# Crossing from the up projection to the down projection: where four activation blocks are loaded, and in which order the down projection's loads are issued

## Chip, cores and metric

The kernel runs on one core of a Trainium2 chip. The metric is the device time of one execution in microseconds (us). A core has five engines, each with its own instruction stream: TensorE (PE, matrix products into PSUM banks), VectorE (DVE), ScalarE (ACT), GpSimd (POOL) and SyncE (SP, here only a queue that issues DMAs). ACT issues some DMAs as well. Engines wait for one another by semaphores; within a stream instructions go in order.

## The reference

One layer of a streaming encoder on 1088 tokens (1024 of a prompt and 64 of a running stream): a mixer of latent attention and gated linear attention, a residual, and then the multilayer perceptron, with which this change has to do:

```python
h2 = rms_norm(x, g_norm2) * (1 + scale2) + shift2
x = x + gate2 * (jnp.square(jax.nn.relu(h2 @ w_up)) @ w_down)
```

`w_up` is 1024 x 4096, `w_down` 4096 x 1024, all in float32.

## The kernel before

**Arithmetic.** Both projections are done as seven products of half-size blocks in place of eight (a Strassen scheme). The seven products are numbered 0 to 6; the four blocks of a matrix are named 11, 12, 21 and 22. Each float32 operand is split into a high and a low part (`split`, lines 100 to 102: ACT casts the high part at L101, another engine, mostly DVE, subtracts it to get the low part at L102), and a product is three matmuls: high by high, high by low, low by high (`mm3`, lines 91 to 95).

**Up projection** (`up`, from line 1531). The 2048 rows of a half are done in 16 blocks of 128 (`j`). Block `j` has seven products of two token halves (272 columns each) and twelve matmuls per half, in the order 0, 1, 2, 5, 3, 4, 6 from `j` = 2 on. ReLU and square are applied and the seven activation combinations that the down projection needs are stored to DRAM (`keep_act`, line 1526), as `u_d[product, j]`, each 128 x 544 floats (272 KB). The stores of block 15 are issued by ACT, those of all others by SP. The activation tiles `st` come from a pool of six places, `sq_`, used in turn; the sums and differences are tiles `sc` from a pool of two places. `AH[j]` and `AL[j]` hold the split token operands of the up products; the places of `AH[0]`, `AL[0]`, `AH[1]`, `AL[1]` carry the tags `ah0`, `al0`, `ah1`, `al1` and outlive the stage.

**Down projection** (`down`, from line 1737). The products come in the order 0, 2, 3, 6, 1, 5, 4, each in 16 steps `(i, j)`, 112 steps in all. A step is 24 matmuls of 272 columns (four row blocks, two token halves, three matmuls) and needs an operand set `opers`: the split weights W (128 x 512) and the split activations U (128 x 544). There are four places for sets: `ah1`, `al1`, and two in the stage's own pool, so the set of step n can be made only when step n-4 is done. W comes out of a quad, four steps' weights in one load of 1 MB (`load_quad`, L1614); U is one 272 KB load of `u_d[i, j]` (`load_u`, L1619) into a ring of eight tiles `ru` that lies where the `st` tiles were. The first four sets need quad (11, 0) and `u_d[0, 0]` to `u_d[0, 3]`. Product 2 uses W = 12 - 22 + 11, so DVE makes 16 differences (`differences`, L105) and 16 sums (L1724) before it; `residual` (L1687) loads four residual blocks `e`, to which `out` (L1776) adds the products.

**What sets the order.** The program text is written by `interleave` (line 46): several generators run against a counted time, and the first in the list that is able goes on. In the up stage the list is `norm2, weights, tokens, up, ahead`; `ahead` (line 1629) writes the first loads and splits of the down projection. Its list in the down stage is `loads, operands, differences, down`. `loads` (line 1680) names, for each quad and residual, the step after which it is written; `PLACES` (line 1669) says where each quad lies. The compiler's scheduler then puts each engine's instructions in order by readiness, in a model of the machine, and may issue a load before others written ahead of it. `tc.keep_in_program_order(x)` takes this freedom away: x is issued behind the instruction that was written before it for the same engine.

Of the kernel before, what the change touches and what calls it, by code (L numbers as in the profile page):

```python
# [10 lines left out]
F32 = mybir.dt.float32  # L11
# [8 lines left out]
P = 128  # L20
# [11 lines left out]
HT = TOK // 2  # L32
# [39 lines left out]
def layer(ctx: ExitStack, tc: tile.TileContext, I, O):  # L72
# [149 lines left out]
    def has(*keys):  # L222
        return lambda: all(k in done or k in groups for k in keys)
# [1164 lines left out]
    with ExitStack() as uctx:  # L1388
# [9 lines left out]
        sq_ = pool("sq", 6)  # L1398
# [212 lines left out]
        def load_quad(x, q, t):  # L1611
            kh, nh = x // 10 - 1, x % 10 - 1
            r0 = 16 * P * kh + 4 * P * q
            SP.dma_start(t, I["w_down"][r0:r0 + 4 * P, 512 * nh:512 * nh + 512].rearrange("(j p) n -> p j n", p=P))  # L1614
            for j in range(4):
                quads[x, 4 * q + j] = t[:, j]

        def load_u(i, j, t, eng=SP):
            eng.dma_start(t, u_d[i, j])  # L1619
            ru[i, j] = t  # L1620

        def split_set(i, j, o, w):

# [5 lines left out]
        def ahead():  # L1629

            yield 0, 0, has("p 15 0")
            for j in range(2):
                load_u(0, j, sq_.tile([P, HT], F32, name="st"), ACT)
            load_quad(11, 0, keep.tile([P, 4, 512], F32, name="quad", tag="ah0"))
            yield 0, 0, has("p 15 1")
            load_quad(11, 1, keep.tile([P, 4, 512], F32, name="quad", tag="al0"))
            yield 0, 3000, None
            for j in range(2):
                split_set(0, j, keep.tile([P, D + TOK], F32R, name="opers", tag=("ah1", "al1")[j]), quads[11, j])
                yield 0, 1000, None  # L1640
# [5 lines left out]
    with ExitStack() as dctx:  # L1646

        PRODUCTS = (0, 2, 3, 6, 1, 5, 4)  # L1650
        STEPS = [(i, j) for i in PRODUCTS for j in range(16)]
        def pool(name, bufs=1):
            return dctx.enter_context(tc.tile_pool(reuse_waits="tile", name=name, bufs=bufs))

        ep = pool("ep")
        E = [ep.tile([P, 4, HT], F32, name=f"e{i}") for i in range(4)]
        rp = pool("rp", 8)
        sp_ = pool("sp")
        def new_quad(n):

            if n in ("x11", "x12"):
                return keep.tile([P, 4, 512], F32, name="quad", tag=n)
            return qp_.tile([P, 4, 512], F32, name="quad", tag=f"quad{n}")

        for _ in range(8):
            rp.tile([P, HT], F32, name="ru")
        opers = [sp_.tile([P, D + TOK], F32R, name="opers", tag=f"set{n}") for n in range(2)]
        qp_ = pool("qp_")
        PLACES = {11: (None, None, 3, 4), 12: (5, 6, 7, 8), 22: (0, 1, 2, "x11"), 21: (5, 6, 7, 8)}
        for n in range(9):  # L1670
            qp_.tile([P, 4, 512], F32, name="quad", tag=f"quad{n}")

        PLACE = {"22": (1, 4), "11": (0, 0), "12": (0, 4), "21": (1, 0)}

        ADDS = {0: ("11", False), 2: ("12", False), 3: ("22", False), 6: ("21", True), 1: ("22", True), 5: ("12", True),
                4: ("11", True)}
        OUT = {c: E[n] for n, c in enumerate(("11", "12", "22", "21"))}
        SPANS = ((0, 0, 512), (1, 512, HT))

        def loads():  # L1680

            def quad(x, q):
                load_quad(x, q, new_quad(PLACES[x][q]))

            def residual(c):
                th, m0 = PLACE[c]
                SP.dma_start(OUT[c], x2_d[:, m0:m0 + 4, HT * th:HT * th + HT])  # L1687

            quad(11, 2)
            for (i, j), what in (((0, 1), (11, 3)), ((0, 3), (12, 0)), ((0, 4), (22, 0)), ((0, 6), "11"), ((0, 8), (12, 1)),  # L1690
# [3 lines left out]
                yield 0, 0, has(f"dn {i} {j}")  # L1694
                if isinstance(what, str):
                    residual(what)
                else:
                    quad(*what)

        def differences():  # L1700

            for j in range(16):
                yield 0, 600, lambda: (12, j) in quads and (22, j) in quads
                sub(quads[12, j], quads[22, j], quads[12, j], DVE)
                done.add(f"diff {j}")

        def operands():
            n_u = 2
            part = {}
            for n, (i, j) in enumerate(STEPS):  # L1710
                while n_u < len(STEPS) and n_u < n + 7:
                    load_u(*STEPS[n_u], rp.tile([P, HT], F32, name="ru"))
                    n_u += 1
                if n < 2:
                    continue
                if n == 2:
                    yield 0, 2500, None
                if n >= 4:
                    yield 0, 600, has("dn %d %d" % STEPS[n - 4])
                x = {0: 11, 2: 11, 3: 12, 6: 21, 1: 11, 5: 22, 4: 21}[i]  # L1720
                yield 0, 0, lambda: (x, j) in quads and (i != 2 or f"diff {j}" in done)
                w = quads[x, j]
                if i == 2:
                    DVE.tensor_tensor(out=w, in0=w, in1=quads[12, j], op=ALU.add)  # L1724
                elif i == 6:
                    if j % 4 == 0:
                        part["t4"] = new_quad("x12")
                    w = part["t4"][:, j % 4]
                    sub(w, quads[21, j], quads[11, j], DVE)
                elif i == 1:  # L1730
                    sub(w, quads[22, j], w, DVE)
                o = (keep.tile([P, D + TOK], F32R, name="opers", tag=("ah1", "al1")[n % 4]) if n % 4 < 2 else
                     sp_.tile([P, D + TOK], F32R, name="opers", tag=f"set{n % 4 - 2}"))
                split_set(i, j, o, w)
                yield 0, 1500, None

        def down():
            banks = {}
            for i in PRODUCTS:
                if i in (0, 1, 4):  # L1740
                    banks.clear()
                late = (14, 15) if i == 4 else (15,)
                for j in range(late[0]):
                    yield 0, 0, lambda: (i, j) in sets
                    for m in range(4):
                        for h in range(2):
                            part(banks, i, j, m, h)
                            yield 375, 0, None
                    done.add(f"dn {i} {j}")
                for m in range(4):  # L1750
                    for h in range(2):
                        for j in late:
                            yield 0, 0, lambda: (i, j) in sets
                            part(banks, i, j, m, h)
                            yield 375, 0, None
                        out(i, m, h, banks[m, h])
                for j in late:
                    done.add(f"dn {i} {j}")

        def part(banks, i, j, m, h):  # L1760
            if (m, h) not in banks:
                banks[m, h] = bank()[:, 0:HW]
            wh, wl, uh, ul = sets[i, j]
            ms, hs = slice(m * P, m * P + P), HALVES[h]
            first = i in (0, 1, 4)
            mm3(banks[m, h], wh[:, ms], wl[:, ms], uh[:, hs], ul[:, hs], first and j == 0, j == 15, not first)

        def out(i, m, h, b):

            c, end = ADDS[i]  # L1770
            th, m0 = PLACE[c]
            e = OUT[c][:, m]
            for s, c0, c1 in SPANS:
                c0, c1 = max(c0, h * HW), min(c1, h * HW + HW)
                if c0 < c1:
                    DVE.scalar_tensor_tensor(out=e[:, c0:c1], in0=b[:, c0 - h * HW:c1 - h * HW],  # L1776
                                             scalar=modT[:, 5, m0 + m, s:s + 1], in1=e[:, c0:c1], op0=ALU.mult, op1=ALU.add)
            if h and end:
                SP.dma_start(O["y_T"][(m0 + m) * P:(m0 + m + 1) * P, HT * th:HT * th + HT], e)

        interleave([loads(), operands(), differences(), down()])


# [60 lines left out]
```

## Time and profile before

| | us |
|---|---|
| three runs: lowest, median, highest | 1432.69, 1434.76, 1436.42 |
| the profiled execution, its own time | 1434.8 |
| its span, first to last instruction | 1433.0 |
| PE busy | 1354.2 (95%) |
| DVE busy | 873.9 (61%) |
| ACT busy | 655.5 (46%) |

The profile gives, for one execution, what every engine did when. "Busy" of PE counts a matmul at whatever clock it ran at. In a timeline each row is a start, a duration, an engine and a line, and in brackets the idle time ahead of it and what ended that. A wait on several things is put down to the last. The granted clock (PEclk) is a share of TensorE's full 2.4 GHz.

### The profile page before, as it was taken

The page shows a single profiled execution, that of the slowest core. Times are in us where ns is not written, and L with a number is a line of the kernel's source. Part 1 is how long each engine was busy: PE and PEld are TensorE (multiplying, and loading weights), DVE is VectorE, ACT ScalarE, POOL GpSimd, SP SyncE. Part 2 cuts the span into 40 slices and gives each one's busy share as a digit, 9 for nine tenths or more (in the row PEclk, how much of TensorE's full clock was granted, in tenths as well). Part 3 has the DMA queues.
Part 4 walks back from the last instruction along what each step waited for, and adds up shares of the span by engine and source line. Part 5 has one row for each costly group of instructions (what it writes and reads, how often), then busy time and mean ns, then how long its engine had stood idle before and what let it go on. Part 6 is the DMA issues. An engine that isn't in the chain of part 4 may idle for free.

```text
span 1433.0 us, 26460 instructions
## 1 busy us (share of the span) xinstructions
PE 1354.2 (95%) x10014; PEld 1268.7 (89%) x10014; DVE 873.9 (61%) x1894; ACT 655.5 (46%) x1623; POOL 273.1 (19%) x388
## 2 busy tenths in 40 slices
PE   6988899978999999999979999999997999999998
PEld 5887778877866779899968999999996999999998
DVE  5688787236455756645399566556533866774554
ACT  5455554334335666644365444444433343334332
POOL 3255445113131211014663000000000000000000
PEclk9999999999999999999988999999998999999999
DMA  9320021474244441264315444444248945433441
GB/s 347 103 71 9 16 80 49 134 210 120 87 141 131 141 130 59 70 188 130 113 32 172 147 155 138 133 152 152 96 159 301 340 135 157 148 116 104 126 124 38
DMA packets 165594, 188.17 MB, mean 131 GB/s; under 512 B 16814, under 2 KB 116442, under 8 KB 165466
## 3 DMA queue, kind: packets, MB, share of 16 engines
q1 hardware_dynamic: 157722, 180.34, 39.6%
q10 hardware_dynamic: 7744, 6.13, 1.3%
q8 instruction: 79, 1.29, 0.4%
q14 instruction: 49, 0.40, 0.1%
HBM read 132.97 MB, written 53.46 MB: 130 GB/s over the span
## 4 chain that ended last, share of the span: by engine, by line
PE 76%; DVE 10%; DMA 5%; ACT 3%; POOL 3%; issue 2%; SPq 0%; DVEq 0%; ACTq 0%; POOLq 0%
PE mm L93 13%; PE mm L94 13%; PE mm L95 13%; PE g L93 5%; PE g L95 5%; PE g L94 5%; PE mm L964 3%; PE tp L93 3%; PE tp L95 3%; PE tp L94 3%; PE g L991 2%; PE mm L166 2%; DMA raw<-in_w_in 1%; PE tp L1001 1%; DMA gv<-mix_d 1%
## 5 line engine op out<-in xcount | busy, mean ns | idle before, releaser
L101 ACT CAST opers<-quad 128x512 fp32r<-128x512 f32 x112 | 69.5, 620 | 191.6 <-PE mm L95 176.8
L102 DVE TENSOR_TENSOR opers<-quad,opers 128x512 fp32r<-128x512 f32 x112 | 77.2, 689 | 116.0 <-ACT opers L101 116.0
L93 PE MATMUL mm<-opers 128*128 128x272 f32 x448 | 128.9, 289 | 9.9 <-ACT opers L101 9.9
L95 PE MATMUL mm<-opers 128*128 128x272 f32 x448 | 129.7, 290 | 0.0
L94 PE MATMUL mm<-opers 128*128 128x272 f32 x448 | 129.3, 289 | 0.4 <-DVE opers L102 0.4
L93 PE MATMUL mm<-ah,wh 128*128 128x272 f32 x424 | 123.7, 293 | 6.2 <-ACT st L1565 6.2
L95 PE MATMUL mm<-ah,wl 128*128 128x272 f32 x424 | 123.5, 292 | 1.1 <-POOL wl L102 1.1
L94 PE MATMUL mm<-al,wh 128*128 128x272 f32 x424 | 123.5, 292 | 0.0
L93 PEld LDWEIGHTS mm<-opers 128*128 128x128 f32 x448 | 85.0, 190 | 10.4 <-ACT opers L101 10.4
L93 PE MATMUL mm<-hh,wh 128*128 128x384 f32 (+2 forms) x264 | 90.7, 347 | 0.5 <-ACT hh L101 0.5
L94 PE MATMUL mm<-hl,wh 128*128 128x384 f32 (+2 forms) x264 | 87.7, 333 | 0.0
L93 PEld LDWEIGHTS mm<-ah,wh 128*128 128x128 f32 x424 | 82.0, 194 | 6.4 <-ACT st L1565 6.4
L95 PE MATMUL mm<-hh,wl 128*128 128x384 f32 (+2 forms) x264 | 87.2, 331 | 0.0
L94 PEld LDWEIGHTS mm<-opers 128*128 128x128 f32 x448 | 84.8, 189 | 0.6 <-DVE opers L102 0.6
L95 PEld LDWEIGHTS mm<-opers 128*128 128x128 f32 x448 | 85.1, 190 | 0.0
L95 PEld LDWEIGHTS mm<-ah,wl 128*128 128x128 f32 x424 | 81.4, 192 | 1.3 <-POOL wl L102 1.3
L94 PEld LDWEIGHTS mm<-al,wh 128*128 128x128 f32 x424 | 81.7, 193 | 0.0
L102 DVE TENSOR_TENSOR opers<-ru,opers 128x544 fp32r<-128x544 f32 x110 | 79.0, 719 | 1.0 <-ACT opers L101 0.9
L101 ACT CAST wh<-ru 128x512 fp32r<-128x512 f32 x67 | 41.2, 619 | 70.9 <-PE g L94 26.0
L101 ACT CAST opers<-ru 128x544 fp32r<-128x544 f32 x110 | 70.6, 643 | 4.5 <-PE mm L95 3.6
L93 PE MATMUL mm<-wh,hh 128*128 128x264 f32 (+3 forms) x216 | 65.8, 305 | 1.6 <-ACT wh L213 1.6
L94 PE MATMUL mm<-wl,hh 128*128 128x264 f32 (+3 forms) x216 | 64.8, 300 | 1.0 <-DVE wl L105 0.9
(415 smaller groups left out, 4436.0 us busy)
## 6 DMA issues: line engine op xcount, KB each, us to landing
ru<-u_d SPq DMA_DIRECT2D x110, 272.0 KB, 2.7
raw<-in_w_ada SPq DMA_DIRECT2D x40, 512.0 KB, 3.8
ru<-in_w_up SPq DMA_DIRECT2D x32, 512.0 KB, 4.0
quad<-in_w_down SPq DMA_DIRECT2D x16, 1024.0 KB, 5.8
u_d<-st SPq DMA_DIRECT2D x60, 272.0 KB, 2.1
u_d<-sc SPq DMA_DIRECT2D x45, 272.0 KB, 2.2
raw<-in_w_in SPq DMA_DIRECT2D x22, 256.0 KB, 3.3
x<-in_xo_T SPq DMA_DIRECT2D x8, 544.0 KB, 5.0
```

Of the source, the lines that this page charges most:

```text
L93: PE.matmul(out, lhsT=ah, rhs=bh, start=first, stop=False, skip_group_check=more)
L94: PE.matmul(out, lhsT=ah, rhs=bl, start=False, stop=False, skip_group_check=more)
L95: PE.matmul(out, lhsT=al, rhs=bh, start=False, stop=last, skip_group_check=more)
L101: ACT.copy(hi, src)
L102: eng.tensor_tensor(out=lo, in0=src, in1=f32(hi), op=ALU.subtract)
L166: mm = PE.matmul(acc[32 * j:32 * j + 32, 0:256], lhsT=scT[:, k, :], rhs=was[k][:, 256 * j:256 * (j + 1)], start=(k == 0), stop=(k == KT - ...
L964: PE.matmul(sp[:n, :w], lhsT=x[:, hd, :n], rhs=y[:, hd, :w], start=(j == 0), stop=(j == 4))
L991: PE.matmul(op[:n, 0:P], lhsT=pt[:kw, k, :n], rhs=kvs[kt // 4].v[:kw, kt % 4, hd], start=(kt == 0), stop=(kt == nkt - 1))
L1001: PE.transpose(tp[:kw, k, :n], pr[k0 // 4][:n, P * k:P * k + kw], ident[:n, :n])
```

## The change

`load_quad` and `load_u` return the DMA. `ahead` no longer loads U of the first two steps by ACT into `st` tiles; it loads U of the first four by SP into the four quarters of one tile `u4` in the place `al0`, right behind quad (11, 0). Quad (11, 1), which lay in `al0`, goes to place 3, (11, 2) to place 4, and (11, 3) to `al0` after `u4`. All other loads of the down projection are kept in program order, and some are written after other steps than before. The ring of `ru` starts with step 4, and the counted pause of 2500 ahead of the split of step 2 goes.

```diff
         def load_quad(x, q, t):
             kh, nh = x // 10 - 1, x % 10 - 1
             r0 = 16 * P * kh + 4 * P * q
-            SP.dma_start(t, I["w_down"][r0:r0 + 4 * P, 512 * nh:512 * nh + 512].rearrange("(j p) n -> p j n", p=P))
+            dma = SP.dma_start(t, I["w_down"][r0:r0 + 4 * P, 512 * nh:512 * nh + 512].rearrange("(j p) n -> p j n", p=P))
             for j in range(4):
                 quads[x, 4 * q + j] = t[:, j]
-
-        def load_u(i, j, t, eng=SP):
-            eng.dma_start(t, u_d[i, j])
+            return dma
+
+        def load_u(i, j, t):
             ru[i, j] = t
+            return SP.dma_start(t, u_d[i, j])
...
             yield 0, 0, has("p 15 0")
-            for j in range(2):
-                load_u(0, j, sq_.tile([P, HT], F32, name="st"), ACT)
             load_quad(11, 0, keep.tile([P, 4, 512], F32, name="quad", tag="ah0"))
-            yield 0, 0, has("p 15 1")
-            load_quad(11, 1, keep.tile([P, 4, 512], F32, name="quad", tag="al0"))
-            yield 0, 3000, None
+            u4 = keep.tile([P, 4, HT], F32, name="u4", tag="al0")
+            for j in range(4):
+                load_u(0, j, u4[:, j])
+            yield 0, 3000, has("p 15 1")
...
-            if n in ("x11", "x12"):
+            if n in ("x11", "x12", "al0"):
                 return keep.tile([P, 4, 512], F32, name="quad", tag=n)
...
-        PLACES = {11: (None, None, 3, 4), 12: (5, 6, 7, 8), 22: (0, 1, 2, "x11"), 21: (5, 6, 7, 8)}
+        PLACES = {11: (None, 3, 4, "al0"), 12: (5, 6, 7, 8), 22: (0, 1, 2, "x11"), 21: (5, 6, 7, 8)}
...
             def quad(x, q):
-                load_quad(x, q, new_quad(PLACES[x][q]))
+                tc.keep_in_program_order(load_quad(x, q, new_quad(PLACES[x][q])))
 
             def residual(c):
                 th, m0 = PLACE[c]
-                SP.dma_start(OUT[c], x2_d[:, m0:m0 + 4, HT * th:HT * th + HT])
-
-            quad(11, 2)
-            for (i, j), what in (((0, 1), (11, 3)), ((0, 3), (12, 0)), ((0, 4), (22, 0)), ((0, 6), "11"), ((0, 8), (12, 1)),
-                                 ((0, 10), (22, 1)), ((0, 13), (12, 2)), ((0, 15), (22, 2)), ((2, 2), (12, 3)),
+                tc.keep_in_program_order(SP.dma_start(OUT[c], x2_d[:, m0:m0 + 4, HT * th:HT * th + HT]))
+
+            quad(11, 1)
+            for (i, j), what in (((0, 1), (11, 2)), ((0, 4), (11, 3)), ((0, 5), (12, 0)), ((0, 6), (22, 0)), ((0, 7), "11"),
+                                 ((0, 9), (12, 1)),
+                                 ((0, 11), (22, 1)), ((0, 13), (12, 2)), ((0, 15), (22, 2)), ((2, 2), (12, 3)),
                                  ((2, 4), (22, 3)), ((2, 7), "12"), ((2, 12), "22"), ((3, 3), (21, 0)), ((3, 7), (21, 1)),
                                  ((3, 11), (21, 2)), ((3, 15), (21, 3)), ((6, 4), "21")):
...
         def operands():
-            n_u = 2
+            n_u = 4
             part = {}
             for n, (i, j) in enumerate(STEPS):
                 while n_u < len(STEPS) and n_u < n + 7:
-                    load_u(*STEPS[n_u], rp.tile([P, HT], F32, name="ru"))
+                    tc.keep_in_program_order(load_u(*STEPS[n_u], rp.tile([P, HT], F32, name="ru")))
                     n_u += 1
                 if n < 2:
                     continue
-                if n == 2:
-                    yield 0, 2500, None
```

## Rows read from the trace of the kernel before

**Rows 1.** Stretches: length, busy (instructions) of PE, PEld, DVE, ACT, POOL; clock, DMA.
```profile
1059.40:1080.30 20.90, 20.90 (x168) 20.79 (x167) 7.33 (x14) 8.14 (x17) 0.00 (x0) 1.00 0.62 213
1080.30:1100.60 20.30, 10.00 (x50) 9.44 (x50) 6.83 (x11) 3.10 (x5) 0.00 (x0) 0.66 1.03 384
...
1110.00:1160.00 50.00, 50.00 (x404) 50.00 (x403) 44.73 (x78) 19.62 (x34) 0.00 (x0) 1.00 0.86 302
1160.00:1400.00 240.00, 240.00 (x1930) 240.00 (x1930) 143.25 (x252) 94.02 (x161) 0.00 (x0) 1.00 0.41 125
```

**Rows 2.** Waits of PE from 1030 us on: total, times, longest.
```profile
PE mm L93 <- ACT opers L101: 9.9, 2, 8.4
```

**Rows 3.** Timeline of PE at the crossing.
```profile
1080.12 0.29 PE L95 MATMUL g<-ah,wl 128*128 128x272 f32 x1
1088.80 1.05 PE L93 MATMUL mm<-opers 128*128 128x272 f32 x3 [8.39 <-ACT opers L101]
...
1095.37 0.39 PE L93 MATMUL mm<-opers 128*128 128x272 f32 x1 [1.54 <-ACT opers L101]
...
1100.59 0.29 PE L93 MATMUL mm<-opers 128*128 128x272 f32 x1
```

**Rows 4.** Timeline of ACT and its DMA issues (ACTq) at the crossing.
```profile
1067.86 0.62 ACT L101 CAST opers<-quad 128x512 fp32r<-128x512 f32 x1 [0.26 <-DMA quad<-in_w_down]
...
1077.73 0.61 ACT L101 CAST opers<-quad 128x512 fp32r<-128x512 f32 x1
...
1079.74 0.33 ACTq L1529 DMA_DIRECT2D u_d<-sc  x1
1080.16 0.40 ACTq L1619 DMA_DIRECT2D st<-u_d  x1
...
1087.14 0.33 ACTq L1529 DMA_DIRECT2D u_d<-sc  x1
1087.56 0.50 ACTq L1619 DMA_DIRECT2D st<-u_d  x1
1088.11 0.64 ACT L101 CAST opers<-st 128x544 fp32r<-128x544 f32 x1 [8.70 <-DMA st<-u_d]
```

**Rows 5.** Timeline of SP's DMA issues (SPq) at the crossing.
```profile
1062.61 0.99 SPq L1614 DMA_DIRECT2D quad<-in_w_down  x2
1077.31 0.98 SPq L1614 DMA_DIRECT2D quad<-in_w_down  x2
1086.81 0.37 SPq L1614 DMA_DIRECT2D quad<-in_w_down  x1
1087.82 0.34 SPq L1619 DMA_DIRECT2D ru<-u_d  x1
```

**Rows 6.** Timeline of DVE at the crossing.
```profile
1081.24 0.43 DVE L1551 TENSOR_TENSOR st<-st,g 128x272 f32<-128x272 f32 x1
...
1086.38 0.73 DVE L105 TENSOR_TENSOR sc<-st 128x544 f32<-128x544 f32 x1 [3.48 <-DMA u_d<-sc]
```

**Rows 7.** DMA issues by line, whole span: count, KB each, median us to landing.
```profile
ru<-u_d SPq DMA_DIRECT2D x110, 272.0 KB, 2.7
...
quad<-in_w_down SPq DMA_DIRECT2D x16, 1024.0 KB, 5.8
...
u_d<-sc SPq DMA_DIRECT2D x45, 272.0 KB, 2.2
```

**Rows 8.** Operations on the tiles `ru` and `quad`: shortest, median, longest in ns.
```profile
L101 ACT CAST opers<-ru x110: 637/643/649, 1096.6 to 1418.0; 128x544 fp32r<-128x544 f32 x110
L102 DVE TENSOR_TENSOR opers<-ru,opers x110: 714/718/727, 1097.2 to 1418.7; 128x544 fp32r<-128x544 f32 x110
...
L105 DVE TENSOR_TENSOR quad<-quad x48: 680/683/693, 1112.8 to 1270.7; 128x512 f32<-128x512 f32 x48
```

**Rows 9.** Waits in SP's queue from 1030 us on: total, times, longest.
```profile
SPq L1779 <- DVE e L1776: 37.6, 13, 29.6
...
SPq L1614 <- PE mm L95: 13.7, 1, 13.7
```

## The prediction

> **What bounds the kernel now.** I looked first at stretches of the span, then at what PE waits for in the last third, then at the timelines around that place, engine by engine. The stretches say where there is something to gain. In the last up block PE does 168 matmuls in 20.90 us, 124.4 ns each, at the full clock; from 1110 us to 1400 us it is busy without a gap at the full clock; between them lie 20.30 us with only 50 matmuls, a mean clock of 0.66 (between the levels of 1.2 and 2.4 GHz) and the DMA engines full [rows 1]. PE's waits from 1030 us on come to 9.9 us in two pieces, for ACT's casts of `opers` [rows 2]. So the down projection is bound by PE except at its start, and only there can a change of loads win.
>
> The timeline of PE gives the price of the crossing. The last up matmul starts at 1080.12, so the next could start at 1080.24; step 2 of the down projection starts at 1100.59, after the 48 matmuls of steps 0 and 1 [rows 3]. These take 48 x 0.1244 = 5.97 us at the full clock. 1100.59 - 1080.24 - 5.97 = **14.4 us lost**: 8.6 us until step 0, 1.7 us between steps 0 and 1, and the rest, about 4.1 us, by matmuls at the lower clock after the pauses and a short wait for a low part.
>
> Why the two operands are late stands in ACT's timeline. W of step 0 is cast at 1067.86, 12 us ahead of time. U is loaded at 1080.16 for step 0 and at 1087.56 for step 1, each right behind a store of block 15 [rows 4], although block 0 of `u_d` was written long before. The code explains it: `up` stands ahead of `ahead` and is nearly always able, so the loads are written after all of block 15, and their `st` tiles are taken in turn after that block's last; the second stands in ACT's stream behind the store of the last difference, which ACT can issue only at 1087.14, since DVE waited until 1086.38 for a place of `sc` to be stored [rows 4, 6]. Each load then shares the DMA engines with four 1 MB quads issued by SP from 1077.31 to 1086.81 [rows 4, 5], and the cast waits 8.70 us [rows 4].
>
> **The change, part by part.**
> - *U of steps 0 to 3 in `al0`.* The place comes free with the first product of block 15: the two quads that before went to `ah0` and `al0` were issued from 1062.61 on [rows 5]. Now it is one quad and 4 x 0.28 MB, about as much data, so I take the same time. A quad lands in 5.8 us, a U load in 2.7 us in the median [rows 7]; queued behind one another they should be there by about 1070. Cast and subtraction take 0.64 + 0.72 us for each U [rows 8]; ACT and DVE are busy 8.14 and 7.33 of 20.90 us in that block [rows 1]. Sets 0 and 1 are then whole by some 1073, 7 us before PE wants them. Price on PE: nothing; without this cover, each us of lateness costs one.
> - *What was on ACT.* Two issues of 0.40 and 0.50 us go [rows 4], and SP gets two more (0.34 us each [rows 5]). ACT's casts no longer stand behind loads.
> - *Steps 2 and 3.* Their W was cast from 1077.73 on [rows 4], their U can follow at once. Step 2 is due at 1080.24 + 2.99 = 1083.2 + 2.99 = 1086.2. Bound from above: its U stands on ACT behind the store of the last difference. Without four quads in flight that difference need not wait until 1086.38: stores of `sc` take 2.2 us [rows 7] after 1079.74 [rows 4], so about 1083, and U is whole by 1085.5; price nothing. If the store is as late as before, U is whole at 1088.8, 2.6 us late, and the lower clock adds about 2.1 us (half of the 4.1 above): 4.7 us. I take nothing.
> - *PSUM.* Step 0 uses all eight banks, the seventh part the second `g` bank, at 1080.24 + 6 x 0.373 = 1082.5. DVE empties it at 1081.24 + 0.43 [rows 6]. Two further subtractions of 0.72 us ahead of it [rows 8] would make it 0.6 us late, none 0. I take 0.3.
> - *Quad (11, 1) and the ring of U.* The quad needs the place of `AL[3]`, free four products of 2.99 us after 1062.6 [rows 5], at about 1074.5; before, SP sat 13.7 us at such a head of its queue until 1077.31 [rows 5, 9]. With 5.8 us to land it is there by 1083; step 4 is due at 1092.2 and its set opens at 1083.2. U of step 4 takes the place of an `st` tile that DVE still reads until about 1081.3, that of step 5 waits for a store, about 1086. Landed in 2.7 us [rows 7], both are in time. Price nothing.
> - *Loads pinned and spread.* Bytes don't change. In the first eight steps (23.9 us) go out four quads, a residual and eight U, 7.5 MB or 316 GB/s, below the 384 GB/s that the crossing had [rows 1]. Each later quad is now written nearer to its use. The tightest, (22, 3), is written after step 20, 1143.0; step 28 starts at 1163.9, and one difference, one sum, cast and subtraction are 2.7 us [rows 8]; with 5.8 us to land there are 12 us of cover. The 32 differences and sums come in a thinner stream than before, and in the dense one DVE at 44.73 of 50.00 us cost PE nothing [rows 1]. The dropped pause of 2500 changes only when a split is written. Price nothing.
>
> A gain beyond the 14.4 us is excluded: PE is at its full rate in the rest of the stage. The sum is made against the profiled execution's own 1434.8 us (span 1433.0), which lies at the median of the runs, 1434.76: 1434.8 - 14.4 + 0.3 = **1420.7 us**.
>
> **A rule to weigh.** SP's queue stood from 1063.6 to 1077.31 with one DMA waiting for PE at its head and later ones behind it, and the loads of U came out only at 1087.82 [rows 5, 9]. The Trainium skill (DMA: Bandwidth & Descriptors, section Anatomy of one DMA) says that DMA engines don't wait on semaphores, the issuing sequencer does, ahead of dispatch; the 13.7 us wait agrees. It speaks against pinning: a fixed order can't pass a load that is not ready. By it the sum would be that of rival B, by the covers above it is mine.
>
> **Rivals.**
> - *A: a store on ACT takes the place.* U of step 2 stands behind the last store, at its old time, at the price of 4.7 us worked out above. For it: ACT's stream did just that to step 1. Against: the store was late for want of DMA, and the quads that took it are spread now. 1420.4 + 4.7 = 1425.1 us.
> - *B: the pinned queue is held at its head.* U of step 4 comes as late as SP's first U came before, 1087.82 [rows 5], and with up to 5.8 us to land behind a quad is whole at 1095.0, 2.8 us after 1092.2; with 2.1 us of clock 1425.3 us. For it: the wait of 13.7 us. Against: that queue was also held by loads that are now behind.
> - *C: U comes no earlier.* The four loads in `ahead` are not pinned, so they may still be issued behind block 15. At 1080.2 with 2.7 us to land and 0.64 us of cast, PE starts at 1083.5, 3.3 us late, and with 2.1 us of clock the time is 1425.8; if they meet the old traffic, it is the old 1434.8. Against: in `al0` they depend on no `st` tile, and the quad in that place was issued at 1062.6.
> - *D: slower.* The quads of 12 and 22, now written later, come after their sets are due. DVE goes in order, so a difference that waits holds every later subtraction, and PE stops. There are four groups, (12, q) with (22, q). To lose 14.0 + 4.3 us it takes 4.6 us a group, 2.5 idle and 2.1 of clock; that decides where SP is 12 + 2.5 us behind its program point. With 5 us idle each the cost is 4 x 7.1 = 28.4: 1448.8 us. For it: SP did wait 29.6 us once for DVE's `e` ahead of an output [rows 9], and DVE is the fullest engine but PE there. Against: outputs begin only after product 6, long past these quads.
>
> **How the numbers follow.** My forecast 0.81, A 0.05, B 0.05, C 0.05, D 0.04. 0.3% (4.3 us) is about what a measurement can tell from no change. The forecast, A, B and two fifths of C are faster: 0.93. The rest of C is the same: 0.03. D is slower: 0.04. The forecast's range goes from 1418.3 (all 14.4 us, and a median 2.1 us low, as the lowest of the three runs stood) to 1422.8; it reaches up to A, B and the lower end of C with 1 us for the runs, 1427, and leaves out D and the upper end of C.
>
> **What would show it.** Right: U of steps 0 to 3 issued by SP at about 1063, casts of U by 1071, PE's waits from 1030 us on under 1 us, the clock at 1.00 from 1080 to 1100 with some 163 matmuls, and DMA there below full. A shows as a wait of PE for `opers` at 1086, B at 1092, C at 1080, D from 1120 on with DVE waiting for `quad`. The forecast is wrong if PE waits more than 2 us anywhere in the down projection, or if the end of the up projection moved.

## The result, and the profile after

The changed kernel took 1419.2 us in the median of four runs (1417.71 to 1420.65), the kernel before 1433.72 us beside it (1431.87 to 1436.42): a ratio of 0.9896, with a 95% interval of 0.9876 to 0.9915, so 12 to 18 us less. The forecast was 1420.7 in a range of 1418.3 to 1427.0, and faster. The profiled execution's own time is 1419.29 us with a span of 1417.5 us. All times of this trace lie 1.7 us earlier than those of before at the crossing, since the last up matmul starts at 1078.42 and not at 1080.12 [rows 3]; this must be taken off when the two are compared.

The same stretches as in [rows 1], of the changed kernel:

```profile
1059.40:1080.30 20.90, 20.90 (x170) 20.90 (x169) 8.76 (x16) 10.29 (x21) 0.00 (x0) 1.00 0.67 244
1080.30:1100.60 20.30, 20.30 (x166) 20.30 (x165) 11.07 (x18) 7.95 (x14) 0.00 (x0) 1.00 0.96 322
1100.60:1110.00 9.40, 9.40 (x78) 9.40 (x77) 5.17 (x9) 3.73 (x7) 0.00 (x0) 1.00 1.05 387
1110.00:1160.00 50.00, 49.71 (x400) 49.52 (x399) 43.49 (x76) 18.92 (x33) 0.00 (x0) 1.00 0.73 256
```

The second row is the one to read: 166 matmuls where there were 50, and a granted clock of 1.00 where the mean was 0.66. The DMA engines are still nearly full in it (0.96), and in the third row they are as full as the crossing was before (1.05, 387 GB/s), at no cost to PE. The last row has 49.71 of 50.00, the one new gap. PE's waits from 1030 us on name it:

```profile
PE mm L93 <- DVE e L1775: 0.3, 1, 0.3
```

Instead of 9.9 us for ACT's casts [rows 2], PE waits 0.3 us for DVE to empty a bank. The crossing itself, in PE's timeline, has no gap at all; the last row is the first matmul of step 5, and the row under it the same matmul in the kernel before:

```profile
1078.42 0.29 PE L95 MATMUL g<-ah,wl 128*128 128x272 f32 x1
1078.55 0.29 PE L93 MATMUL mm<-opers 128*128 128x272 f32 x1
...
1093.49 0.29 PE L93 MATMUL mm<-opers 128*128 128x272 f32 x1
```

```profile
1109.55 0.29 PE L93 MATMUL mm<-opers 128*128 128x272 f32 x1
```

ACT's, SP's and DVE's timelines, to be held against [rows 4], [rows 5] and [rows 6]:

```profile
1066.04 0.62 ACT L101 CAST opers<-quad 128x512 fp32r<-128x512 f32 x1
...
1067.04 0.65 ACT L101 CAST opers<-u 128x544 fp32r<-128x544 f32 x1
...
1068.11 0.65 ACT L101 CAST opers<-u 128x544 fp32r<-128x544 f32 x1
...
1077.10 0.63 ACT L101 CAST opers<-u 128x544 fp32r<-128x544 f32 x1
...
1078.40 0.65 ACT L101 CAST opers<-u 128x544 fp32r<-128x544 f32 x1
...
1082.51 0.33 ACTq L1529 DMA_DIRECT2D u_d<-sc  x1
```

```profile
1060.72 0.38 SPq L1614 DMA_DIRECT2D quad<-in_w_down  x1
1061.16 2.01 SPq L1621 DMA_DIRECT2D u<-u_d  x4
...
1072.63 0.38 SPq L1614 DMA_DIRECT2D quad<-in_w_down  x1
1079.69 2.38 SPq L1621 DMA_DIRECT2D ru<-u_d  x5
1086.95 0.84 SPq L1621 DMA_DIRECT2D ru<-u_d  x2
```

```profile
1081.76 0.71 DVE L105 TENSOR_TENSOR sc<-st 128x544 f32<-128x544 f32 x1
```

U of steps 0 and 1 is cast 11 and 13 us ahead of its use, U of steps 2 and 3 right behind its W, and the store of the last difference leaves ACT at 1082.51 instead of 1087.14, because DVE no longer sits for a store ahead of that difference (3.48 us in [rows 6], none in the row above). Where the time went: between the last up matmul and step 5 the crossing lost 14.38 us before and 0.02 us now, 14.4 us; the up projection ended 1.7 us earlier; the 15.5 us between the two executions' own times leave 0.5 us that the rest of the stage, with the new 0.3 us wait, gave back. The 1.7 us can't be put down to the change: the changed kernel itself has its last up matmul at 1078.42 us in this trace and at 1082.77 us in its second one. Over the ten traces of this study that start lies between 1076.95 and 1083.80 us, and both ends belong to kernels with parts of the change. What moves it was not tried.

That spread is larger than some of the effects below. So each experiment is read at two places: its ratio, and the **loss at the crossing**, which is the start of step 5 less that of the last up matmul, less 0.12 us for that matmul and 5 x 2.986 us for steps 0 to 4. For before it is 1109.55 - 1080.12 - 0.12 - 14.93 = 14.38 us.

### The profile page after: what moved, and what is told of

It is laid out like the page before. It is cut to its first block, busy times and chain, and to the rows that moved or that the text cites. A ratio compares the mean times of both kernels' runs of the same rounds, so it can differ in the third digit from the quotient of the medians.

```text
span 1417.5 us, 26453 instructions
## 1 busy us (share of the span) xinstructions
PE 1349.8 (95%) x10014; PEld 1263.6 (89%) x10014; DVE 873.6 (62%) x1894; ACT 655.6 (46%) x1623; POOL 273.1 (19%) x388
## 4 chain that ended last, share of the span: by engine, by line
PE 77%; DVE 10%; DMA 4%; POOL 3%; ACT 3%; issue 2%; SPq 0%; DVEq 0%; POOLq 0%; ACTq 0%
PE mm L93 13%; PE mm L94 13%; PE mm L95 13%; PE g L93 6%; PE g L95 6%; PE g L94 5%; PE mm L964 3%; PE tp L93 3%; PE tp L95 3%; PE tp L94 3%; PE g L991 2%; PE mm L166 2%; DMA raw<-in_w_in 1%; PE tp L1001 1%; DMA gv<-mix_d 1%
```

## The experiments

My theory T: U of steps 0 and 1 was late for two reasons that add up, its issue behind block 15's stores and the four quads on the DMA engines then, and u4 in `al0` alone cures it. Rivals: the pins carry the gain (P), only the lateness or only the traffic counts (L, Q), all four U must be early (F).

**The changed kernel again**, beside the next three.

> The changed kernel once more, beside the next three. Theory T (the 14 us were lost because U of steps 0 and 1 was issued late and then shared the DMA engines with four quads; both are gone): 14 to 15 us below the kernel before, a ratio of 0.990, PE waiting under 1 us after 1030 us and the clock at 1.00 through the crossing. Rival N (part of the first gain was luck of the runs): 0.993 or more.

Ratio 0.9903 (0.9882 to 0.9923), medians 1422.28 and 1434.69 us, loss at the crossing 0.02 us. The gain is there again: 13.9 us by the ratio and 12.4 by the medians, a bit under the 14 to 15 that I expected, with 14.36 us less lost at the crossing as before. The two intervals overlap, and N falls.

**Without the pins.**

```diff
-                tc.keep_in_program_order(load_quad(x, q, new_quad(PLACES[x][q])))
+                load_quad(x, q, new_quad(PLACES[x][q]))
...
-                tc.keep_in_program_order(SP.dma_start(OUT[c], x2_d[:, m0:m0 + 4, HT * th:HT * th + HT]))
+                SP.dma_start(OUT[c], x2_d[:, m0:m0 + 4, HT * th:HT * th + HT])
...
-                    tc.keep_in_program_order(load_u(*STEPS[n_u], rp.tile([P, HT], F32, name="ru")))
+                    load_u(*STEPS[n_u], rp.tile([P, HT], F32, name="ru"))
```

> The changed kernel without any of the three pins; places, u4 and the points at which the loads are written stay. Theory T with u4 as the part that counts: quads come out ahead of the ring's U again, three of them from about 1075 us on, but U of steps 0 to 3 landed by 1070 and step 4 is due only 12 us after the crossing, so the time stays within 2 us of the changed kernel: 1418 to 1421. Rival P (the pins carry the gain, since three quads of 1 MB take 8 us of DMA time ahead of U of step 4): U of step 4 is whole about 3 us late, with the lower clock 5 us: 1424, PE waiting for opers at step 4.

Ratio 0.9903 (0.9884 to 0.9922), median 1422.15 us: the same as with pins (1.2 us above the 1418 to 1421 expected, but so was the changed kernel beside it). But the trace has the mechanism of rival P, in small. SP's and ACT's timelines and PE's, in this order:

```profile
1077.24 1.65 SPq L1614 DMA_DIRECT2D quad<-in_w_down  x3
1082.87 13.15 SPq L1621 DMA_DIRECT2D ru<-u_d  x11
```

```profile
1092.39 0.64 ACT L101 CAST opers<-ru 128x544 fp32r<-128x544 f32 x1 [4.05 <-DMA ru<-u_d]
```

```profile
1093.09 0.39 PE L93 MATMUL mm<-opers 128*128 128x272 f32 x1 [0.80 <-ACT opers L101]
1093.85 0.39 PE L94 MATMUL mm<-opers 128*128 128x272 f32 x1 [0.37 <-DVE opers L102]
```

Three quads come out first, U of step 4 lands only for a cast at 1092.39, and PE loses 1.71 us at step 4 (not the 5 us of P). The pins remove this; 1.7 us of 1420 can't be told in the ratio, so their worth is shown by the traces alone, here and in the next experiment.

**u4 alone**: the edit above, and the points of the kernel before.

```diff
-            for (i, j), what in (((0, 1), (11, 2)), ((0, 4), (11, 3)), ((0, 5), (12, 0)), ((0, 6), (22, 0)), ((0, 7), "11"),
-                                 ((0, 9), (12, 1)),
-                                 ((0, 11), (22, 1)), ((0, 13), (12, 2)), ((0, 15), (22, 2)), ((2, 2), (12, 3)),
+            for (i, j), what in (((0, 1), (11, 2)), ((0, 3), (11, 3)), ((0, 3), (12, 0)), ((0, 4), (22, 0)), ((0, 6), "11"), ((0, 8), (12, 1)),
+                                 ((0, 10), (22, 1)), ((0, 13), (12, 2)), ((0, 15), (22, 2)), ((2, 2), (12, 3)),
```

> As e1, and the loads written at the points of the kernel before, so that of the change only u4 in al0 with the places that it needs is left. Theory T with u4 as the part that counts: 1418 to 1421. Rival P: 1424 or more, as in e1, and more DMA traffic between 1080 and 1110.

Ratio 0.9902 (0.9882 to 0.9922), median 1421.45 us (0.5 above the range expected), loss 1.78 us, again at step 4. u4 with its places is worth 12.6 of the 14.4 us by itself. P falls.

**Pins and spread points alone.** The changed kernel with `ahead`, the places of quads 11 and the start of the ring as before; of its edit:

```diff
+            for j in range(2):
+                load_u(0, j, sq_.tile([P, HT], F32, name="st"), ACT)
...
-            u4 = keep.tile([P, 4, HT], F32, name="u4", tag="al0")
-            for j in range(4):
-                load_u(0, j, u4[:, j])
-            yield 0, 3000, has("p 15 1")
+            yield 0, 0, has("p 15 1")
+            load_quad(11, 1, keep.tile([P, 4, 512], F32, name="quad", tag="al0"))
+            yield 0, 3000, None
...
-            quad(11, 1)
+            quad(11, 2)
```

> The kernel before with pins and the spread points alone: U of steps 0 and 1 are again loaded by ACT into st tiles, quads (11, 0) and (11, 1) in ah0 and al0. Theory T: the four quads leave the crossing, so the store of the first sum takes 2.2 us instead of 6.6 and the loads land in 2.7 us instead of 7.5; U of step 0 is still issued at 1080.2, PE starts at about 1083.6, 3.3 us late, and loses about 2 us by the lower clock; U of step 1 lands at about 1086.7, near its time: 5 to 7 us lost of 14.4, 1424 to 1427. Rival L (only the late issue counts, traffic doesn't): 1431 to 1434. Rival Q (only traffic counts): 1419 to 1421.

Ratio 0.9968 (0.9954 to 0.9982), median 1430.75 us, loss 8.54 us. By the time alone this is a miss: it lies 3.8 us above my 1424 to 1427, just under the range of L, and the interval reaches into that range. The crossing decides: L would have left nearly all of the 14.4 us, Q next to nothing, and the 8.54 us are 1.5 over my 5 to 7. PE's timeline has the last up matmul and the first of step 5:

```profile
1083.80 0.29 PE L95 MATMUL g<-ah,wl 128*128 128x272 f32 x1
...
1107.39 0.29 PE L93 MATMUL mm<-opers 128*128 128x272 f32 x1
```

ACT's timeline shows what I had left out:

```profile
1083.77 0.44 ACTq L1621 DMA_DIRECT2D st<-u_d  x1
...
1087.73 0.52 ACTq L1621 DMA_DIRECT2D st<-u_d  x1
1088.29 0.64 ACT L101 CAST opers<-st 128x544 fp32r<-128x544 f32 x1 [5.21 <-DMA u_d<-st]
1094.01 0.65 ACT L101 CAST opers<-st 128x544 fp32r<-128x544 f32 x1 [5.07 <-DMA st<-u_d]
```

The last up matmul starts at 1083.80 here, and the first load goes out at that time. It lands after 3.3 us, but its cast stands in ACT's stream behind the second load and starts only when that one is issued (1087.73 + 0.52). The second then competes with the ring, of which SP issued three U between 1085.98 and 1087.07 and a fourth at 1089.72, and with the stores of block 15, and takes 6 us. Fewer quads alone let other loads in.

**Two U in `al0`, with and without pins.** Ring from step 2; the second kernel also has the first edit of this section.

```diff
-            for j in range(4):
+            for j in range(2):
                 load_u(0, j, u4[:, j])
...
-            n_u = 4
+            n_u = 2
```

> The changed kernel with only two U in al0, those of steps 0 and 1; the ring starts with step 2, pins and spread points stay. Theory T (four is more than the pinned order needs): U of step 2 can be issued once DVE has read the last st tile at about 1081, is whole at 1085.5 and due at 1086.2; U of step 3 is about 0.4 us late: ratio 0.990, PE waiting under 1.5 us in all. Rival F (all four must be early): the ring is held by the stores of block 15, PE waits 3 us or more at step 2 or 3 and the ratio is 0.993 or more.

> Two U in al0 and no pins. Theory T (the pins matter only where the ring is due soon): four quads come out ahead of the ring as in the kernel before, U of step 2 is issued between 1083 and 1088, lands 3 to 8 us later and is due at 1086.2: PE waits 3 to 9 us at step 2 and loses 2 us by the lower clock, 0.994 to 0.998. Rival U (pins never matter, U of steps 0 and 1 alone counts): 0.990, PE waiting under 1.5 us.

With pins the ratio is 0.9901 (0.9874 to 0.9928) and the loss 1.6 us; without, 0.9965 (0.9950 to 0.9979) and 10.0 us. PE's timeline at step 2, first with pins, then without:

```profile
1084.86 0.64 PE L93 MATMUL mm<-opers 128*128 128x272 f32 x3 [1.25 <-ACT opers L101]
```

```profile
1092.84 1.05 PE L93 MATMUL mm<-opers 128*128 128x272 f32 x3 [7.04 <-ACT opers L101]
```

So F falls for the pinned order (PE waited 1.25 us for U and 0.3 for `e`, just over the 1.5 expected), and without pins U falls. The number of early U and the pins cover for one another: with four early, the ring is first due at step 4, and quads ahead of it cost 1.7 us; with two, it is due at step 2, six microseconds sooner, and the loss with quads ahead is 10 us, 8.4 more than with pins.

**u4 late.** The four loads are issued by ACT, in program order, so behind block 15's last store.

```diff
-        def load_u(i, j, t):
+        def load_u(i, j, t, eng=SP):
             ru[i, j] = t
-            return SP.dma_start(t, u_d[i, j])
+            return eng.dma_start(t, u_d[i, j])
...
-                load_u(0, j, u4[:, j])
+                tc.keep_in_program_order(load_u(0, j, u4[:, j], ACT))
```

> The changed kernel with the four loads into al0 issued by ACT in program order, so behind the last store of block 15, at about 1084 on the clock of the kernel before; quads pinned and spread as in the changed kernel. Theory T: with little traffic U of step 0 lands after 3 to 4 us, PE starts 7 to 8 us late and loses about 2 us by the lower clock; the later steps follow without a wait: 9 to 10 us lost, a ratio of 0.996 to 0.998. Rival Q (traffic is the larger part): 0.993 or less.

Ratio 0.9980 (0.9964 to 0.9996), loss 12.74 us against my 9 to 10. ACT's and PE's timelines, and the stretches with the columns of [rows 1]:

```profile
1083.58 0.33 ACTq L1529 DMA_DIRECT2D u_d<-sc  x1
1083.95 2.57 ACTq L1621 DMA_DIRECT2D u<-u_d  x4
1089.18 1.36 ACT L101 CAST opers<-u 128x544 fp32r<-128x544 f32 x2 [9.88 <-DMA u<-u_d]
```

```profile
1080.01 0.29 PE L95 MATMUL g<-ah,wl 128*128 128x272 f32 x1
1089.88 0.59 PE L93 MATMUL mm<-opers 128*128 128x272 f32 x1 [9.58 <-ACT opers L101]
...
1095.56 0.43 PE L93 MATMUL mm<-opers 128*128 128x272 f32 x1
...
1107.80 0.29 PE L93 MATMUL mm<-opers 128*128 128x272 f32 x1
```

```profile
1084.00:1088.00 4.00, 0.00 (x0) 0.00 (x0) 0.00 (x0) 0.00 (x0) 0.00 (x0) 0.50 0.96 350
1088.00:1092.00 4.00, 2.12 (x9) 2.09 (x10) 2.03 (x3) 2.46 (x4) 0.00 (x0) 0.50 1.03 377
1092.00:1096.00 4.00, 4.00 (x19) 4.00 (x19) 0.86 (x2) 0.32 (x2) 0.00 (x0) 0.50 1.01 370
1096.00:1100.00 4.00, 4.00 (x33) 4.00 (x33) 1.63 (x3) 1.93 (x4) 0.00 (x0) 0.98 0.56 186
```

PE stands from 1080.01 + 0.12 to 1089.88: 9.7 us, where I had 7 to 8. Then 19 matmuls in 4 us at a clock of 0.50 where 33 fit at 0.98: step 0 takes 5.68 us (1089.88 to 1095.56), 2.7 more than its 2.99, and step 1 another 0.3. No quad is in this traffic until 1091.26 (the two before were issued by 1075), but ring loads and stores fill the DMA engines all the same, and the four loads take 5 us to land. So Q falls. The 12.74 us are not the price of the old issue without the quads, though: the first load goes out 3.9 us after the last up matmul here, and right at it in the kernel before. Nearest to that price is the 8.54 us with pins alone, where the first load goes out right at it too.

**Old points, pinned.** The edit of "u4 alone", on the changed kernel.

> The changed kernel with the loads written at the points of the kernel before, but pinned. Theory T (spreading has cover of its own and is worth nothing here): ratio 0.990, PE waiting under 1 us after 1030 us. Rival S (several quads together delay the ring's U): a wait of PE of 2 us or more between steps 5 and 12, 0.992 or more.

Ratio 0.9891 (0.9864 to 0.9919), loss 0.01 us, PE waiting 0.3 us for `e`. What T says of the spread holds: spreading the loads over later steps is worth nothing by itself once they are pinned.

Side by side, by the same reading of PE's timeline:

| U of the first steps | quads | last up matmul | step 5 | loss, us | ratio |
|---|---|---|---|---|---|
| two in `st`, late | free, old points (before) | 1080.12 | 1109.55 | 14.38 | 1 |
| two in `st`, late | pinned, spread | 1083.80 | 1107.39 | 8.54 | 0.9968 |
| four in `al0`, late | pinned, spread | 1080.01 | 1107.80 | 12.74 | 0.9980 |
| two in `al0`, early | free, spread | 1079.54 | 1104.63 | 10.04 | 0.9965 |
| two in `al0`, early | pinned, spread | 1077.34 | 1094.00 | 1.61 | 0.9901 |
| four in `al0`, early | free, old points | 1076.95 | 1093.78 | 1.78 | 0.9902 |
| four in `al0`, early | free, spread | 1080.05 | 1096.81 | 1.71 | 0.9903 |
| four in `al0`, early | pinned, old points | 1082.25 | 1097.31 | 0.01 | 0.9891 |
| four in `al0`, early | pinned, spread (changed) | 1078.42 | 1093.49 | 0.02 | 0.9896 |
| the same, again | pinned, spread | 1082.77 | 1097.84 | 0.02 | 0.9903 |

The two columns agree: 1.6 us of loss less go with a ratio of 0.998, 4 to 6 us with 0.996 to 0.997, and 12 to 14 us with 0.989 to 0.990; each saving lies inside the interval of its ratio.

## Why the prediction was right

- **The size.** The forecast took the 14.4 us lost at the crossing as the whole of what could be won, and 0.3 us back. The trace shows 14.36 us won, a clock of 1.00 through the crossing and one new wait of 0.3 us, in a place that I hadn't named (the first bank of product 2, held until DVE has added what product 0 left there to `e`). The 0.3 us of the sum were meant for another wait, which didn't come (PSUM, below); that the two are equal is luck. 1434.8 - 14.1 = 1420.7 lay 1.5 us above the first median and 1.6 us below the second: within what the end of the up projection moves from run to run. I had named a moved end as a sign that the forecast is wrong. It did move, by 1.7 us, but the 4.35 us between two traces of the changed kernel show that one trace of each can't carry this sign.
- **The cause.** Both halves of it are borne out, but they don't add up as I thought. Early U alone wins 12.6 us, pins and spread points alone 5.8, together 14.4. With U late, more than half of the loss stays even when no quad is in the way: 8.5 us where the first load goes out as the up projection ends, 12.7 us where it goes out 3.9 us later. With U early, quads in the way cost 1.7 us. The late issue was the cause. The traffic made it worse, and is not only the quads': ring and stores take their place. The sign of a DMA share below full came only just, with 0.96, and was not what the gain needed.
- **U in `al0`.** Forecast: issued at about 1063 and landed by 1070. Issued from 1061.16, and U of steps 0 and 1 cast at 1067.04 and 1068.11, on a clock 1.7 us earlier; U of steps 2 and 3 was cast only at 1077.10 and 1078.40, behind its W, which was in time. The step holds; each load took 5.5 to 6.0 us to land behind the quad, where the 2.7 us of [rows 7] is the median of loads with a freer queue.
- **PSUM, 0.3 us.** It was 0.0: DVE emptied the second `g` bank at 1079.54 + 0.43 and took the low part of U behind that, from 1079.89, as these rows of its timeline show; the bank was due at about 1080.8.

```profile
1079.54 0.43 DVE L1551 TENSOR_TENSOR st<-st,g 128x272 f32<-128x272 f32 x1
1079.89 0.71 DVE L102 TENSOR_TENSOR opers<-u,opers 128x544 fp32r<-128x544 f32 x1
```

- **Steps 2 to 5.** Quad (11, 1) was forecast for 1074.5 and the ring's first U for 1081.3; they were issued at 1072.63 and 1079.69, which is 1074.3 and 1081.4 on the clock of before. U of step 5, put at about 1086 behind a store, went out right behind that of step 4. Nothing was late.
- **Pins and spread at no price.** Right for the change as a whole. The forecast didn't say what the pins themselves were worth; the trace without them says 1.7 us with four early U and 8.4 us with two. The spread is worth nothing that shows. The new wait for `e`, 0.3 to 0.4 us, stands in all five traces that have both the pins and U in `al0`, and in none of the others; whether the pins cause it was not tried.
- **The rule.** The Trainium skill (DMA: Bandwidth & Descriptors, section Anatomy of one DMA, which is on GpSimd's path) has the issuing sequencer wait ahead of dispatch, and I weighed it as a case against a fixed order. The rule itself holds in these traces too, where SP and ACT issue: ACT's cast in the experiment with pins alone stood behind a DMA that its sequencer was still holding (1088.29, right behind the load of 1087.73). The pinned queue did stand too, with nothing issued from 1082.07 to 1086.95, at no cost to PE. Against the pins the rule had no force, since what a free order put first, 1 MB quads not due for 12 us or more, did more harm than a load that was not ready.
- **Rivals.** A's mechanism, a cast behind a store on ACT, is what the first U met with pins alone; the changed kernel escapes it, as the store leaves at 1082.51 and U of step 2 was cast at 1077.10, ahead of it. B's late ring came without the pins, not with them. C near its full price is the experiment with u4 late, 12.7 of 14.4 us. Nothing spoke for D: DVE waited 2.0 us in all for quads, and PE never for those of 12 and 22.
- **A term that was too small.** I priced a pause's lower clock at 2.1 us. The kernel before paid 1.9 and 2.2 us, the latter with a wait of 0.37 us for a low part; with u4 late it was 3.0 us over two steps, and without pins and with two U 2.8 us. None of this came into the forecast's sum, but the expectations for these two experiments were short by 0.8 to 1 us of it.

## What to carry to other kernels

At a seam between two stages, look for the small load that the first instruction of the new stage waits for, and give it a place that is free before the old stage's last results are: a place from the old stage's own ring comes free only in that ring's order, however old the data is. Large prefetches that a scheduler finds ready can go ahead of small loads that are due. The early place is the main cure: alone it won 12.6 of 14.4 us here, the fixed order alone 5.8. Where the early place is had, the fixed order is not seen in the total time, so read the loss at the seam.

## What the runs showed of the hardware that was not expected

- The price of the lower clock after a pause is not one figure, and it didn't follow the length of the pause. The first step behind it took longer by 2.7 us after 7.2 us of pause (two U, no pins), by 1.9 after 8.6 (the kernel before) and by 2.7 after 9.7 (u4 late). In the last case the clock was 0.50 through all of step 0 (rows above); in the kernel before it was back during step 0, which ran from 1088.80 to 1093.67, as its stretches show. What decided between them wasn't tried.

```profile
1088.00:1092.00 4.00, 3.20 (x14) 3.17 (x14) 0.73 (x1) 0.64 (x1) 0.00 (x0) 0.50 1.05 408
1092.00:1096.00 4.00, 2.22 (x13) 1.79 (x12) 0.65 (x2) 1.17 (x2) 0.00 (x0) 0.92 1.05 408
```

- Loads and stores of 272 KB filled the DMA engines as well as quads did: in the experiment with u4 late the DMA share was 0.96 and 1.03 in the stretches from 1084 to 1092 us, with no quad issued between 1075 and 1091.
